# Hybrid attention block: key tile 3 of the stick-breaking heads in two fp32r products, the last 16 keys in one stacked product, three merge gates ahead of the first branch product

## The chip, the core and the metric

The kernel runs on one core of a Trainium2 chip. The metric is the device time of one execution in microseconds (us). The engines are named as in the profile: PE (TensorE, matrix products; PEld are its weight loads), DVE (VectorE), ACT (ScalarE), POOL (GpSimd), SP (SyncE, which issues most DMAs). SBUF is the on-chip memory, PSUM the accumulators that PE writes.

## What is computed

One decoder block on 512 tokens of width 1024, with 16 meta tokens put in front (L = 528): a layer norm, one wide projection, eight differential attention heads, sixteen stick-breaking heads, a SiLU gate on each, two branch products merged by sigmoid gates, an output projection, and a residual with layer norm. Cut to what the change touches:

```python
proj = jnp.einsum('bld,dn->bln', h, w_in[i])
q_d, k_d, v_d, g_d, q_s, k_s, v_s, g_s, m_d, m_s = jnp.split(proj, IN_OFFSETS, axis=-1)

# differential head: ALiBi bias, two softmaxes, a = p0 - lam * p1
s = jnp.einsum('bhcqd,bhckd->bhcqk', q, k) * (DIFF_HEAD_DIM ** -0.5)
p = jax.nn.softmax(jnp.where(dist >= 0, s + alibi, -jnp.inf), axis=-1)
a = p[:, :, 0] - lam * p[:, :, 1]
y_d = jnp.einsum('bhqk,bhkd->bhqd', a, v)

# stick-breaking head
z = jnp.einsum('bhqd,bhkd->bhqk', q, k) * (SB_HEAD_DIM ** -0.5)
log_keep = jnp.where(before, jax.nn.log_sigmoid(-z), 0.0)
suffix = lax.cumsum(log_keep, axis=3, reverse=True) - log_keep
a = jnp.where(before, jnp.exp(jax.nn.log_sigmoid(z) + suffix), 0.0)
y_s = jnp.einsum('bhqk,bhkd->bhqd', a, v)

br_d = jnp.einsum('blw,wd->bld', y_d * jax.nn.silu(g_d), w_br_diff[i])
br_s = jnp.einsum('blw,wd->bld', y_s * jax.nn.silu(g_s), w_br_sb[i])
merged = jax.nn.sigmoid(m_d + b_gate[i, 0]) * br_d + jax.nn.sigmoid(m_s + b_gate[i, 1]) * br_s
y = jnp.einsum('bld,de->ble', merged, w_out[i])
```

## The kernel before

**Two forms of a product.** Most fp32 operands are split into a rounded high part and the rest, both of type fp32r, and a product is the sum of two or three fp32r products, one pass over the array each (high by high, high by low, low by high). Operands that stay plain fp32 need no split and one product, which the profile lists as two passes.

**Stages.** After the start (layer norm, the normed input transposed into `hTh` and `hTl`), the work runs in 16 units: eight differential heads ("d"), then eight pairs of stick-breaking heads ("s", heads c = 0 and 1 of a pair). While a unit's attention runs, PE projects keys, values and queries of the units after it (`proj_pos` L370, `proj_tok` L356 to L358) and in the s units also two gates. Weights come as 512 KB blocks, each split into `wh` (ACT, L97) and `wl` (DVE, L103) two projections ahead, in the order of the list `seq`. A d unit takes some 24 us, an s unit some 38 us.

**One head.** Scores (`logits`, L495 and L501) go to two PSUM slots. In a stick-breaking head DVE adds a mask to the score in PSUM (L639), ACT takes two sigmoids (L642, L643), DVE runs a scan and a product into `apad` (L645, L646). The four query tiles see 144, 272, 400 and 528 keys. `transposed` turns the attention matrix on PE (L514, L519) in three PSUM tiles, and ACT and DVE split it (L524, L525) into `ta[0]` to `ta[2]`: 512, 416 and 288 query columns for key tiles 0 to 2. Key tile 3 (160 columns, `ta[3]`) and the last 16 keys (32 columns, `ta[4]`) are copied as plain fp32. `values` (L471 to L487) turns the values likewise: `V` for tiles 0 to 2, `vf` for tile 3, `v4` for the last 16.

**Products with the values.** A differential head (`d_values`) has three fp32r products for each of tiles 0 to 2 and one fp32 product each for tile 3 (L598) and the last keys (L599). In a stick-breaking head (`s_values`) the high and the low part of the 64 value columns stand side by side in the 128 stationary columns of `V[c]`, so one product gives both halves, and two products (high and low attention) do for a tile: L654 and L661 for tile 0, L659 and L660 for tiles 1 and 2. The fp32 products of tile 3 (L655) and of the last keys (L656) have 64 stationary columns. The two halves are then added (L663, L664).

**The merge.** When the units are done, both gated results are split into `ghd`, `gld`, `ghs`, `gls` (16 casts on ACT, L728, 16 subtractions on DVE, L729). Then, for each of eight output blocks: a merge gate or two (`merge_gate`, a projection of `hTh`/`hTl`), the two branch products, and the merging. Before block 0, the merge gates (0,0), (1,0) and (0,1) run in the last unit, and (1,1) and (0,2) in the loop ahead of the first branch product. The loads of `eg`, `eb` and `hr` and the work on them (L748 to L754) are written behind the loop.

**What sets the order.** The functions hand out steps with nominal times; a scheduler then orders the instructions on each engine, by its own model and the tiles' dependences. On the chip each engine runs its list in order, so the first instruction that waits holds up all behind it.

Of the kernel before, what the change touches and what calls it, by code (L numbers as in the profile page):

```python
# [16 lines left out]
P = 128  # L17
# [26 lines left out]
def hybrid_block_kernel(ctx: ExitStack, tc: tile.TileContext, x, meta, emb_g, emb_b, w_in, b_gate,  # L44
# [127 lines left out]

    dist = const.tile([P, L], F32, name="dist")
    g.iota(dist, pattern=[[-1, L]], base=400, channel_multiplier=1, allow_small_or_imprecise_dtypes=True)
    g.affine_select(dist, dist, pattern=[[-1, L]], compare_op=ALU.is_ge, fill=1e30, base=400, channel_multiplier=1)
# [237 lines left out]
    with tc.tile_pool(name="att", bufs=1) as ap:  # L413
# [6 lines left out]
        v4s = []  # L420
        for n in range(2):
            v4 = ap.tile([P, P], F32, name=f"v4{n}")
            g.memset(v4, 0.0)
            v4s.append(v4)
# [41 lines left out]
        def values(unit, kind, parity):  # L466
# [19 lines left out]
            pe.transpose(t4[:M, :P], vT[:, 512:528], ident)  # L486
            v.tensor_copy(v4[:M], t4[:M, :P])  # L487
            unit["V"] = V, vf, v4

# [21 lines left out]
        def transposed(ta, a):  # L511
# [9 lines left out]
            def split(t, w, n):  # L521
                h = ap.tile([P, w], F32R, tag=f"ah{n}", name=f"ah{n}")
                l = ap.tile([P, w], F32R, tag=f"al{n}", name=f"al{n}")
                s.copy(h, t[:, :w])  # L524
                v.tensor_tensor(l, t[:, :w], h.bitcast(F32), op=ALU.subtract)  # L525
                return h, l
# [7 lines left out]
            def part1():  # L534
# [6 lines left out]
                ta[4] = ap.tile([P, 32], F32, tag="af4", name="af4")  # L541
                s.copy(ta[4], t1[:, 416:448])

            def part2():
# [7 lines left out]
                ta[3] = ap.tile([P, 160], F32, tag="af3", name="af3")  # L552
# [287 lines left out]
```

## Time and profile before

| | us |
|---|---|
| runs: median (lowest, highest of 3) | 752.0 (751.91, 752.81) |
| profiled execution | 751.83 |
| its span, first to last instruction | 750.1 |

The profile shows one execution. The table below is its page's view of busy time and the number of instructions of the engines.

| engine | busy us | instructions |
|---|---|---|
| PE | 733.0 | 4390 |
| PEld | 651.4 | 4390 |
| DVE | 543.7 | 1181 |
| ACT | 413.2 | 983 |
| POOL | 85.2 | 106 |

How to read the rows that follow in the prediction. A row of the timeline gives start and length in us, engine, line of the code, operation, tiles written and read, for a matmul "rows*columns" of the stationary operand and the shape that streams, and a count where rows are merged; in brackets stands idle time of the engine before the row and what ended it. A row of a group gives the count, then busy time in all and the mean of one in ns, then idle time before. A row of the windows gives the stretch, its length, the busy time of PE, PEld, DVE, ACT and POOL, then the granted clock, the DMA share and GB/s. The mean clock granted to PE was 0.993.

### The profile page before, as it was taken

To read this page: it belongs to the slowest core of one execution; us is meant where nothing else is said; L and a number is where in the kernel's file an instruction comes from. 1 tells how busy PE (TensorE), PEld (TensorE's weight loads), DVE (VectorE), ACT (ScalarE), POOL (GpSimd) and SP (SyncE) were. 2 spreads that over 40 slices of the span, in tenths; PEclk is the share of its full clock that TensorE was granted. 3 is DMA by queue.
4 is the path that set the end of the run, shared out by engine and by line. 5 is a ranking of instruction groups with operands and counts; after the bars stand their busy time and mean duration, and the time that the engine had idled before them with its cause. 6 is when DMAs were issued, how large, how long until landed. Compare 5 with 4: busy or idle time off the path is not lost.

```text
span 750.1 us, 11849 instructions
## 1 busy us (share of the span) xinstructions
PE 733.0 (98%) x4390; PEld 651.4 (87%) x4390; DVE 543.7 (72%) x1181; ACT 413.2 (55%) x983; POOL 85.2 (11%) x106
## 2 busy tenths in 40 slices
PE   7999999999999999999999999999999999999996
PEld 6899999999999979898989898988878888888885
DVE  6888898888887789695969596967478343335555
ACT  6476777676777787575647474746473232324200
POOL 5510110111000000000000000001001000000101
PEclk8999999999999999999999999999999999999998
DMA  8132112121212121212222222122244333325221
GB/s 260 32 114 85 57 57 85 57 81 51 68 57 86 56 85 39 75 57 85 57 84 58 84 57 85 57 86 57 84 168 142 110 87 102 95 85 195 86 85 57
DMA packets 105340, 63.90 MB, mean 85 GB/s; under 512 B 2065, under 2 KB 100530, under 8 KB 105282
## 3 DMA queue, kind: packets, MB, share of 16 engines
q1 hardware_dynamic: 104098, 58.93, 26.6%
q10 hardware_dynamic: 1184, 4.20, 1.6%
q8 instruction: 35, 0.57, 0.3%
q14 instruction: 23, 0.19, 0.1%
HBM read 61.03 MB, written 2.10 MB: 84 GB/s over the span
## 4 chain that ended last, share of the span: by engine, by line
PE 90%; DVE 5%; ACT 3%; DMA 1%; issue 1%; POOL 0%; SPq 0%; DVEq 0%; ACTq 0%; POOLq 0%
PE ps L370 23%; PE ps L357 14%; PE ps L358 14%; PE ps L356 14%; PE sc L501 5%; PE t L514 3%; PE pso L782 2%; PE pso L781 2%; PE pso L780 2%; PE t L519 1%; PE av L659 1%; DMA raw<-in_w_in_dram 1%; PE tv L471 1%; PE av L655 1%; DVE hTl L239 1%
## 5 line engine op out<-in xcount | busy, mean ns | idle before, releaser
L103 DVE TENSOR_TENSOR wl<-raw,wh 128x512 fp32r<-128x512 f32 x187 | 131.5, 732 | 63.5 <-ACT wh L97 63.3
L97 ACT CAST wh<-raw 128x512 fp32r<-128x512 f32 x192 | 109.8, 621 | 120.8 <-PE ps L357 111.0
L370 PE MATMUL ps<-hTh,wh 128*128 128x264 f32 x512 | 147.5, 288 | 0.5 <-ACT k L452 0.4
L370 PE MATMUL ps<-hTl,wh 128*128 128x264 f32 x512 | 146.4, 286 | 0.0
L370 PE MATMUL ps<-hTh,wl 128*128 128x264 f32 x512 | 146.3, 286 | 0.0
L356 PE MATMUL ps<-hTh,wh 128*128 128x512 f32 x368 | 144.7, 393 | 0.0
L357 PE MATMUL ps<-hTl,wh 128*128 128x512 f32 x368 | 144.4, 392 | 0.0
L358 PE MATMUL ps<-hTh,wl 128*128 128x512 f32 x368 | 144.3, 393 | 0.0
L370 PEld LDWEIGHTS ps<-hTh,wh 128*128 128x128 f32 x512 | 96.5, 188 | 2.6 <-ACT k L452 0.9
L370 PEld LDWEIGHTS ps<-hTl,wh 128*128 128x128 f32 x512 | 96.6, 189 | 1.1
L370 PEld LDWEIGHTS ps<-hTh,wl 128*128 128x128 f32 x512 | 96.5, 188 | 0.0
L358 PEld LDWEIGHTS ps<-hTh,wl 128*128 128x128 f32 x368 | 69.1, 188 | 13.9
L357 PEld LDWEIGHTS ps<-hTl,wh 128*128 128x128 f32 x368 | 69.2, 188 | 13.2
L356 PEld LDWEIGHTS ps<-hTh,wh 128*128 128x128 f32 x368 | 69.2, 188 | 13.0
L645 DVE TENSOR_TENSOR_SCAN om<-om 128x528 f32<-128x528 f32 (+2 forms) x64 | 55.1, 868 | 9.9 <-ACT om L642 9.1
L501 PE MATMUL sc<-k,A 128*128 128x264 f32 (+2 forms) x256 | 54.1, 305 | 0.0
L525 DVE TENSOR_TENSOR al<-t,ah 128x512 fp32r<-128x512 f32 (+2 forms) x72 | 39.7, 571 | 19.5 <-PE av L661 12.2
L524 ACT CAST ah<-t 128x512 fp32r<-128x512 f32 (+2 forms) x72 | 34.8, 504 | 17.1 <-PE t L514 16.6
L642 ACT ACTIVATE om<-sc 128x264 f32<-128x264 f32 (+3 forms) x80 | 31.7, 397 | 21.1 <-DVE sc L639 20.2
L501 PEld LDWEIGHTS sc<-k,A 128*128 128x128 f32 x256 | 39.7, 189 | 2.5
L514 PE MATMUL t<-ident,apad 128*128 128x128 f32 x240 | 40.9, 272 | 0.7 <-DVE apad L646 0.7
L583 ACT ACTIVATE e<-e,mn 128x528 f32<-128x528 f32 (+3 forms) x64 | 37.0, 578 | 8.1 <-DVE mn L579 7.6
(210 smaller groups left out, 1340.3 us busy)
## 6 DMA issues: line engine op xcount, KB each, us to landing
raw<-in_w_in_dram SPq DMA_DIRECT2D x80, 512.0 KB, 3.8
raw<-in_w_br_diff_dram SPq DMA_DIRECT2D x8, 512.0 KB, 3.7
raw<-in_w_br_sb_dram SPq DMA_DIRECT2D x8, 512.0 KB, 3.8
rawo<-in_w_out_dram SPq DMA_DIRECT2D x8, 512.0 KB, 3.5
hr<-in_x_dram ACTq DMA_DIRECT2D x4, 512.0 KB, 6.8
out_dram<-hr SPq DMA_DIRECT2D x8, 256.0 KB, 2.0
xt<-in_x_dram SPq DMA_DIRECT2D x3, 512.0 KB, 8.8
xt<-in_x_dram SPq DMA_DIRECT2D x2, 256.0 KB, 3.4
```

Source lines behind the costliest of these rows:

```text
L97: s.copy(split[n][0][:, o, :], raws[n][:, o, :])
L103: eng.tensor_tensor(wl[:, o, :], raws[n][:, o, :], wh[:, o, :].bitcast(F32), op=ALU.subtract)
L356: pe.matmul(ps, wh[:, k, :], hh[:, k, o:], start=(k == 0), stop=False)
L357: pe.matmul(ps, wh[:, k, :], hl[:, k, o:], start=False, stop=False)
L358: pe.matmul(ps, wl[:, k, :], hh[:, k, o:], start=False, stop=(k == KT - 1))
L370: pe.matmul(ps[:, :H2], a[:, k, :], b[:, k, ts(c, H2)], start=(k == 0 and m == 0), stop=(k == KT - 1 and m == 2))
L501: pe.matmul(ps[:, :n], q, K[:, m, k0:k0 + n], start=(m == 0), stop=(m == 1))
L514: pe.transpose(t[:, o:o + P], a[:, AOFF[i] + j * P:AOFF[i] + (j + 1) * P], ident)
L524: s.copy(h, t[:, :w])
L525: v.tensor_tensor(l, t[:, :w], h.bitcast(F32), op=ALU.subtract)
L583: s.activation(e[c], e[c], AF.Exp, scale=-1.0, bias=m[:, 0:1], accum_out=zs[:, i, c:c + 1])
L645: v.tensor_tensor_scan(rev, rev, rev, 1.0, ALU.mult, ALU.min)
```

## The change

**Stick-breaking heads, key tile 3.** `V[c]` gets a fourth tile of 128 keys, `vf` goes away; the 160 columns of attention are split like the others (`ta[3]` is a pair), and the loop over tiles in `s_values` runs over 1 to 3. The fp32 product becomes two fp32r products.

**The last 16 keys, all heads.** Instead of `v4` and `af4` in fp32, there are stacked fp32r tiles: in `a4` the high part of the 16 attention rows stands in rows 0 to 15 and the low part in rows 32 to 47 (for d heads the high part again in rows 64 to 79), in `v4` the matching parts of the values, zeros between. One fp32r product over 128 rows sums them. `tails` holds a pair of tiles for the d heads and one for each c, cleared once.

**Merge gates.** `MERGE` lists them by block: (1,1), (0,2), (1,2) ahead of the first branch products, then two a block up to block 5, none for blocks 6 and 7. The list of weights follows it.

**Biases.** The distance matrix `dist` is no longer kept: the bias of head 0 is built in place, and each later bias is half the one before it.

```diff
+    MERGE = [[(1, 1), (0, 2), (1, 2)]] + [[(0, j + 2), (1, j + 2)] for j in range(1, 6)] + [[], []]
     for j in range(8):
-        seq += [(m, i) for m, i in (("ms", j + 1), ("md", j + 2)) if i < 8]
+        seq += [("m" + "ds"[c], i) for c, i in MERGE[j]]
         seq += [("bd", j), ("bs", j)]
...
+        tails = {}
+        for n in ("d", 0, 1):
+            tails[n] = (ap.tile([P, P], F32R, name=f"v4{n}"), ap.tile([P, 32], F32R, name=f"a4{n}"))
+            for t in tails[n]:
+                g.memset(t.bitcast(F32), 0.0)
...
-            V = [ap.tile([P, 3, P], F32R, tag=f"v{c}", name=f"V{c}") for c in range(2)]
-            vf = ap.tile([P, P], F32, tag="vf", name="vf")
-            v4 = v4s[parity]
+            V = [ap.tile([P, 4, P], F32R, tag=f"v{c}", name=f"V{c}") for c in range(2)]
+            t4 = ptp.tile([P, 512], F32, tag="tp", name="t4")[:M, :P]
+            pe.transpose(t4, vT[:, 512:528], ident)
             if kind == "d":
...
+                v4 = tails["d"][0]
+                s.copy(v4[:M], t4)
+                s.copy(v4[32:32 + M], t4)
+                v.tensor_tensor(v4[64:64 + M], t4, v4[:M].bitcast(F32), op=ALU.subtract)
             else:
                 for c, own, oth in ((0, LO, HI), (1, HI, LO)):
-                    src = tvv[:, :3, own]
+                    src = tvv[:, :, own]
                     s.copy(V[c][:, :, own], src)
                     v.tensor_tensor(V[c][:, :, oth], src, V[c][:, :, own].bitcast(F32), op=ALU.subtract)
-            s.copy(vf, tvv[:, 3, :])
-            t4 = ptp.tile([P, 512], F32, tag="tp", name="t4")
-            pe.transpose(t4[:M, :P], vT[:, 512:528], ident)
-            v.tensor_copy(v4[:M], t4[:M, :P])
+                    v4 = tails[c][0]
+                    s.copy(v4[:M, own], t4[:, own])
+                    s.copy(v4[32:32 + M, own], t4[:, own])
+                    v.tensor_tensor(v4[:M, oth], t4[:, own], v4[:M, own].bitcast(F32), op=ALU.subtract)
...
-                ta[4] = ap.tile([P, 32], F32, tag="af4", name="af4")
-                s.copy(ta[4], t1[:, 416:448])
+                a4, t4 = tails[head][1], t1[:M, 416:448]
+                s.copy(a4[:M], t4)
+                if head == "d":
+                    s.copy(a4[64:64 + M], t4)
+                v.tensor_tensor(a4[32:32 + M], t4, a4[:M].bitcast(F32), op=ALU.subtract)
...
-                ta[3] = ap.tile([P, 160], F32, tag="af3", name="af3")
-                s.copy(ta[3], t2[:, 288:448])
+                if head == "d":
+                    ta[3] = ap.tile([P, 160], F32, tag="ah3", name="af3")
+                    s.copy(ta[3], t2[:, 288:448])
+                else:
+                    ta[3] = split(t2, 160, 3, 288)
...
-            g.tensor_scalar(bias, dist, -(2.0 ** -(h + 1)), None, op0=ALU.mult)
+            if h == 0:
+                g.iota(bias, pattern=[[-1, L]], base=400, channel_multiplier=1, allow_small_or_imprecise_dtypes=True)
+                g.affine_select(bias, bias, pattern=[[-1, L]], compare_op=ALU.is_ge, fill=1e30, base=400,
+                                channel_multiplier=1)
+            g.tensor_scalar(bias, biases[-1] if h else bias, 0.5 if h else -0.5, None, op0=ALU.mult)
...
             pe.matmul(av, V[c][:, 0, :], ta[0][0], start=True, stop=False)
-            pe.matmul(av[own, QOFF[3]:], vf[:, own], ta[3], start=False, stop=False)
-            pe.matmul(av[own, QOFF[4]:], v4[:, own], ta[4], start=False, stop=False)
-            for j in range(1, 3):
+            pe.matmul(av[:, QOFF[4]:], v4, a4, start=False, stop=False)
+            for j in range(1, 4):
                 o = av[:, QOFF[j]:]
                 pe.matmul(o, V[c][:, j, :], ta[j][0], start=False, stop=False)
                 pe.matmul(o, V[c][:, j, :], ta[j][1], start=False, stop=False)
...
     for j in range(8):
-        run([merge_gate(c, i) for c, i in ((1, j + 1), (0, j + 2)) if i < 8])
+        run([merge_gate(c, i) for c, i in MERGE[j]])
```

**The order, place 1: PE, end of a stick-breaking head.** `av` is the head's result in PSUM, `V` its values, `ah` and `al` the split attention, `af` and `vf` the fp32 ones. Before, the products stand in one run:

```order
L655 MATMUL av<-af_5306,vf 64x160
L656 MATMUL av<-af_5291,v_506 64x32
L659 MATMUL av<-ah_5287,V_5000 128x416
L660 MATMUL av<-al_5288,V_5000 128x416
L659 MATMUL av<-ah_5302,V_5000 128x288
L660 MATMUL av<-al_5303,V_5000 128x288
L661 MATMUL av<-al_5275,V_5000 128x512
```

After, the last products of a head; the products of the last keys (`av<-a_510,v_509 128x32`) and of tile 1 stand some 20 projection products further up:

```order
L680 MATMUL av<-ah_4046,V_3738 128x288
L355 MATMUL ps<-hTh,wl 128x512
L367 MATMUL ps<-hTh,wh 128x264
L367 MATMUL ps<-hTl,wh 128x264
L681 MATMUL av<-al_4047,V_3738 128x288
L680 MATMUL av<-ah_4050,V_3738 128x160
L367 MATMUL ps<-hTh,wl 128x264
L681 MATMUL av<-al_4051,V_3738 128x160
L682 MATMUL av<-al_4019,V_3738 128x512
```

The fp32 products with 64 columns are gone, tile 3 comes as two products of 160 columns behind tile 2, and projections stand between them, as each waits for its own split.

**Place 2: DVE, scores of the first head of the fourth stick-breaking unit,** up to the mask of the score of 144 keys (`sc<-sc,om 128x144`), which frees a score slot. `wl` is a weight split, `k` the keys of the next unit, `V` and `v` the values. Before:

```order
L451 TENSOR_TENSOR k_4536<-ps,k_4536 64x264
L645 SCALAR_TENSOR_TENSOR om<-om 128x272
L453 CAST k_4536<-k_4536 64x264
L646 TENSOR_TENSOR apad_496<-sgm,om 128x271
L103 TENSOR_TENSOR wl<-raw,wh 128x512
L508 TENSOR_TENSOR om<-sc,neg 128x144
L103 TENSOR_TENSOR wl<-raw,wh 128x512
L451 TENSOR_TENSOR k_4535<-ps,k_4535 64x264
L639 TENSOR_TENSOR sc<-sc,om 128x144
```

After:

```order
L666 SCALAR_TENSOR_TENSOR om<-om 128x272
L685 TENSOR_TENSOR ysT<-av,half 64x512
L667 TENSOR_TENSOR apad_491<-sgm,om 128x271
L488 TENSOR_TENSOR V_4624<-tv,V_4624 128x4x64
L492 TENSOR_TENSOR v_505<-t_4625,v_505 16x64
L513 TENSOR_TENSOR om<-sc,neg 128x144
L449 TENSOR_TENSOR k_4594<-ps,k_4594 64x264
L104 TENSOR_TENSOR wl<-raw,wh 128x512
L660 TENSOR_TENSOR sc<-sc,om 128x144
```

The addition of the last head's halves (`ysT`), a wider split of the values and the small subtraction for the last keys have come in; one split of weights and one of the keys' subtractions less stand ahead of the mask.

**Place 3: DVE, between the last unit and the merge.** `gld`, `gls` are the low parts of the gated results, `sm` the first merged product, `hr` the residual rows, `wl` the next weights. Before:

```order
L664 TENSOR_TENSOR ysT<-av,half 64x512
L729 TENSOR_TENSOR gld<-ydT,ghd 128x512 x8
L729 TENSOR_TENSOR gls<-ysT,ghs 128x512 x4
L739 TENSOR_TENSOR sm_6429<-ps,sm_6429 128x512
L729 TENSOR_TENSOR gls<-ysT,ghs 128x512 x4
L753 SCALAR_TENSOR_TENSOR hr<-hr,xmv,eg 128x1024
L103 TENSOR_TENSOR wl<-raw,wh 128x512 x3
L753 SCALAR_TENSOR_TENSOR hr<-hr,xmv,eg 128x1024
L103 TENSOR_TENSOR wl<-raw,wh 128x512
```

After:

```order
L685 TENSOR_TENSOR ysT<-av,half 64x512
L750 TENSOR_TENSOR gld<-ydT,ghd 128x512 x8
L750 TENSOR_TENSOR gls<-ysT,ghs 128x512 x6
L774 SCALAR_TENSOR_TENSOR hr<-hr,xmv,eg 128x1024
L750 TENSOR_TENSOR gls<-ysT,ghs 128x512
L760 TENSOR_TENSOR sm_6528<-ps,sm_6528 128x512
L750 TENSOR_TENSOR gls<-ysT,ghs 128x512
L774 SCALAR_TENSOR_TENSOR hr<-hr,xmv,eg 128x1024
L104 TENSOR_TENSOR wl<-raw,wh 128x512 x2
```

One `hr` has moved ahead of the last two `gls`, and two of them stand ahead of the first `wl` instead of one. On PE, 22 projection products stand between the last product with the values and the first one with `ghd`, where there were 11; and 52 products further on, as before, comes the first one with that `wl`.

More of the change, by code (lines that the diff above doesn't have):

```diff
@@ L170, in hybrid_block_kernel @@
     hTl = hpool.tile([P, KT, 48 + L], F32R, tag="hTl", name="hTl")[:, :, 48:]
-    dist = const.tile([P, L], F32, name="dist")
-    g.iota(dist, pattern=[[-1, L]], base=400, channel_multiplier=1, allow_small_or_imprecise_dtypes=True)
-    g.affine_select(dist, dist, pattern=[[-1, L]], compare_op=ALU.is_ge, fill=1e30, base=400, channel_multiplier=1)
     neg = const.tile([P, M + P], F32, name="neg")
@@ L419, in hybrid_block_kernel @@
             apads.append(a)
[L420 to L424, printed above, removed]
+        tails = {}
[3 more added lines that the diff above has]
+                g.memset(t.bitcast(F32), 0.0)
         def stage_q(unit, kind, n):
@@ L464, in stage_v, with values @@
             unit["vT"] = vT
-        def values(unit, kind, parity):
+        def values(unit, kind):
             vT = unit["vT"]
@@ L509, in with_lo, with transposed @@
             return t
-        def transposed(ta, a):
+        def transposed(ta, a, head):
             def full(t, o, i, j):
@@ L551, in part2 @@
                 ta[2] = split(t2, 288, 2)
-                ta[3] = ap.tile([P, 160], F32, tag="af3", name="af3")
-                s.copy(ta[3], t2[:, 288:448])
+                if head == "d":
[3 more added lines that the diff above has]
+                    ta[3] = split(t2, 160, 3, 288)
             return [part0, part1, part2]
+        biases = []
         def d_scores(unit, h):
@@ L562, in d_scores @@
             bias = ap.tile([P, L], F32, tag="bias", name="bias", bufs=2)
-            g.tensor_scalar(bias, dist, -(2.0 ** -(h + 1)), None, op0=ALU.mult)
+            if h == 0:
[3 more added lines that the diff above has]
+            g.tensor_scalar(bias, biases[-1] if h else bias, 0.5 if h else -0.5, None, op0=ALU.mult)
+            biases.append(bias)
             a = apads[h % 2]
@@ L593, in d_values @@
         def d_values(unit, ta):
-            (vh, vl), vf, v4 = unit["V"]
+            (vh, vl), vf = unit["V"]
+            v4, a4 = tails["d"]
             av = pav.tile([P, 512], F32, tag="av", name="av")
@@ L598, in d_values @@
             pe.matmul(av[:, QOFF[3]:], vf, ta[3], start=False, stop=False)
-            pe.matmul(av[:, QOFF[4]:], v4, ta[4], start=False, stop=False)
+            pe.matmul(av[:, QOFF[4]:], v4, a4, start=False, stop=False)
             for j in range(1, 3):
@@ L650, in s_values @@
         def s_values(unit, c, p, ta):
-            V, vf, v4 = unit["V"]
+            V = unit["V"]
+            v4, a4 = tails[c]
             own, oth = ((LO, HI), (HI, LO))[c]
@@ L654, in s_values @@
             pe.matmul(av, V[c][:, 0, :], ta[0][0], start=True, stop=False)
-            pe.matmul(av[own, QOFF[3]:], vf[:, own], ta[3], start=False, stop=False)
-            pe.matmul(av[own, QOFF[4]:], v4[:, own], ta[4], start=False, stop=False)
-            for j in range(1, 3):
+            pe.matmul(av[:, QOFF[4]:], v4, a4, start=False, stop=False)
+            for j in range(1, 4):
                 o = av[:, QOFF[j]:]
@@ L692, in hybrid_block_kernel @@
                 proj.append(stage_q(units[u + 2], *UNITS[u + 2]))
-            steps = pending + [(0.6, lambda unit=unit: values(unit, kind, u % 2))]
+            steps = pending + [(0.6, lambda unit=unit: values(unit, kind))]
             pending = []
@@ L697, in hybrid_block_kernel @@
                 steps += spread(d_scores(unit, n), 0.0, TD[0], 10)
-                parts = transposed(ta, apads[n % 2])
+                parts = transposed(ta, apads[n % 2], "d")
                 steps += [(TD[1] + 0.7 * m, f) for m, f in enumerate(parts)]
@@ L713, in hybrid_block_kernel @@
                     steps += spread(s_scores(unit, c), 4.4 * c + (2.0 if n == 0 and c == 0 else 0.0), 0.85, 5)
-                    parts = transposed(ta, apads[c])
+                    parts = transposed(ta, apads[c], c)
                     steps += [(7.0 + 6.5 * c + 0.7 * m, f) for m, f in enumerate(parts)]
```

15 lines of the change are left out of this document (9 added, 6 removed).

## The prediction

> **What bounds the kernel now.** I read the page first: busy shares, then the chain that ended last.
>
> ```profile
> span 750.1 us, 11849 instructions
> PE 733.0 (98%) x4390; PEld 651.4 (87%) x4390; DVE 543.7 (72%) x1181; ACT 413.2 (55%) x983; POOL 85.2 (11%) x106
> ...
> PE 90%; DVE 5%; ACT 3%; DMA 1%; issue 1%; POOL 0%; SPq 0%; DVEq 0%; ACTq 0%; POOLq 0%
> ```
>
> TensorE is busy for 98% of the span and carries 90% of the chain. Next I asked for the busy time of one stick-breaking unit (two heads, between two value transposes); the columns after the length are PE, PEld, DVE, ACT, POOL.
>
> ```profile
> 318.00:356.00 38.00, 38.00 (x242) 33.99 (x241) 29.36 (x60) 22.99 (x60) 2.84 (x2) 1.00 0.24 70
> ```
>
> PE fills all 38.00 us; DVE has 8.6 us to spare, ACT 15. So the time is the sum of what PE streams, plus a few holes. Durations of matmuls overlap in these rows, so I price a matmul by the distance from its start to the next start.
>
> **Products with the values, stick-breaking heads.** These are the rows of PE's timeline around one head's end: start, length, line, tiles, shape, count.
>
> ```profile
> 385.01 0.39 PE L358 MATMUL ps<-hTh,wl 128*128 128x512 f32 x1
> 385.23 0.39 PE L356 MATMUL ps<-hTh,wh 128*128 128x512 f32 x1
> 385.55 0.49 PE L655 MATMUL av<-af,vf 128*64 128x160 f32 x2
> 385.87 0.25 PE L656 MATMUL av<-af,v 128*64 128x32 f32 x2
> 386.05 0.46 PE L659 MATMUL av<-ah,V 128*128 128x416 f32 x1
> 386.35 0.35 PE L660 MATMUL av<-al,V 128*128 128x416 f32 x1
> 386.54 0.29 PE L659 MATMUL av<-ah,V 128*128 128x288 f32 x1
> ```
>
> A 512-column product takes 0.22 to 0.23 us (385.01 to 385.23), a 416-column one 0.19 (386.35 to 386.54). Without L655 and L656, L659 would start at 385.46 and L660 at 385.65; L660 started at 386.35. The two plain-fp32 products, two passes each, onto 64 output rows, cost **0.70 us a head**, entering and leaving them included. There are 16 heads: the group below counts 32, two passes each.
>
> ```profile
> L655 PE MATMUL av<-af,vf 128*64 128x160 f32 x32 | 7.8, 324 | 0.0
> ```
>
> In their place stand three single-pass products with 128 stationary columns: one of 32 columns (v4 by a4) and two of 160 (tile 3 high and low). The kernel before has no single-pass fp32r product narrower than 256 columns, so their price has to be bounded. The differential heads have a 160- and a 32-column fp32 product with 128 stationary columns, and the transposes are 128 wide:
>
> ```profile
> 77.51 0.28 PE L370 MATMUL ps<-hTh,wl 128*128 128x264 f32 x1
> 77.63 0.43 PE L598 MATMUL av<-af,vf 128*128 128x160 f32 x2
> 77.90 0.30 PE L599 MATMUL av<-af,v 128*128 128x32 f32 x2
> 78.04 0.43 PE L602 MATMUL av<-ah,V 128*128 128x416 f32 x1
> 78.31 0.35 PE L603 MATMUL av<-al,V 128*128 128x416 f32 x1
> ...
> 393.22 0.27 PE L519 MATMUL t<-turned,apad 128*128 128x128 f32 x1
> 393.32 0.27 PE L514 MATMUL t<-ident,apad 128*128 128x128 f32 x1
> 393.35 0.37 PE L501 MATMUL sc<-k,A 128*128 128x264 f32 x1
> ```
>
> From 77.63, where the 264-column product's 0.12 us end, to 78.31 is 0.68; L602 itself is worth 0.19, so the fp32 work of a differential head is 0.49 us: 0.27 for the 160 columns (77.63 to 77.90), 0.22 for the two passes of 32, or 0.11 a pass. The transposes also stand 0.10 to 0.11 apart, whatever little they stream.
> - Lower end: streaming alone. From 264 columns in 0.12 to 512 in 0.225 is 0.42 ns a column, so 160 columns take 0.08, and 32 columns take 0.03, the smallest distance shown (393.32 to 393.35). A head: 0.19.
> - Upper end: a narrow product runs no faster than fp32 in both passes, 0.27 for 160 columns, 0.11 for 32. A head: 0.65.
> - I take 0.11 for all three, the distance of the nearest short products with 128 stationary columns: 0.33 a head.
>
> So a head gains 0.70 - 0.33 = 0.37 us, 16 heads **5.9 us** (from 0.8 to 8.2).
>
> A rule of the Trainium skill would make it more: the page "TensorE: Matmul & The Clock Gate", section "Back-to-back issue gap", gives N/2.4 + 2.5 ns warm, 25 ns for the smallest. By it a head would cost an estimated 0.16 us and the 16 would gain 8.6. The trace does not follow it at 128 columns, where it says 56 ns and the transposes show 110.
>
> **Differential heads.** Tile 3 stays fp32; the last 16 keys become one pass instead of two: 0.22 to 0.11, eight heads, **0.9 us** (0 to 1.5).
>
> **What the vector engines get.** DVE rows by shape: line, tiles, shapes, count, then busy, mean ns.
>
> ```profile
> L525 DVE TENSOR_TENSOR al<-t,ah 128x288 fp32r<-128x288 f32 x24 | 10.8, 451 | 6.9 <-ACT ah L524 6.6
> L639 DVE TENSOR_TENSOR sc<-sc,neg 128x128 f32<-128x128 f32 x48 | 13.6, 289 | 2.5 <-PE sc L501 2.2
> L487 DVE COPY v<-t 16x128 f32<-16x128 f32 x16 | 4.5, 279 | 1.1 <-PE t L486 0.4
> L582 DVE TENSOR_TENSOR mn<-mn 128x1 f32<-128x1 f32 x16 | 2.4, 152 | 0.3
> ```
>
> Per stick-breaking unit DVE gains two subtractions of 160 columns (0.32 each, between 289 and 451 ns), four small ones on 16 rows (0.15 to 0.28 each), 64 more columns in each of two L483 (0.06, at the 1 ns a column between the first two rows), and loses the 0.28 of L487: **1.1 to 1.6 us**. It lies beside PE's 38 us unless the scores wait for it. The tightest place I found is a score product that needs the PSUM slot which ScalarE's second sigmoid reads, itself behind a DVE row:
>
> ```profile
> 368.86 0.29 ACT L643 ACTIVATE sgm<-sc 128x144 f32<-128x144 f32 x1
> ...
> 369.20 0.41 PE L501 MATMUL sc<-k,A 128*128 128x264 f32 x2
> ```
>
> The slot was free at 369.15 and the product started at 369.20: nothing to spare there. What DVE does ahead of that row grows by one 160-column subtraction, the wider L483 and a small subtraction, less L487: 0.32 + 0.12 + 0.2 - 0.28 = 0.4 us, and PE comes 0.37 earlier for each head; but the new order also puts a subtraction of the keys (L451) and a wl behind it. So a unit loses between 0 and 0.8 us; between these I take **0.1 us, 0.8 in eight units**, near the lower end, since the row above shows PE losing nothing with no slack at all. ACT's additions are of the size of small copies and it idles 15 us a unit: 0. A differential unit gets one small subtraction on DVE: 0. On POOL the two instructions that made `dist` leave the start, but POOL's next work there waited for DVE anyway, so nothing comes of it; the halving chain of the biases keeps one instruction per head, and clearing six small tiles is done long before their first use. `t4` now takes its PSUM slot before V is copied; the next user of a slot comes a dozen products later: 0.
>
> ```profile
> L182 POOL TENSOR_TENSOR lne<-xmv,epsr 128x1 f32<-128x1 f32 x4 | 0.8, 190 | 3.9 <-DVE xmv L206 3.8
> ```
>
> Where the heads change kind, two holes remain, filled or widened by the order of the activation-table loads. The new order has as many loads; I leave the holes as they are, 0.7 us either way.
>
> ```profile
> 263.54 0.40 PE L495 MATMUL sc<-k,A 128*128 128x288 f32 x1 [1.22 <-ACT sgm L643]
> ...
> 272.95 0.63 PE L514 MATMUL t<-ident,apad 128*128 128x128 f32 x4 [0.70 <-DVE apad L646]
> ```
>
> **The third merge gate.** Around the first branch product (L356 on ghd):
>
> ```profile
> 548.39 0.58 ACT L663 COPY half<-av 64x512 f32<-64x512 f32 x1 [3.08 <-PE av L661]
> 549.73 4.27 ACT L728 CAST ghd<-ydT 128x512 fp32r<-128x512 f32 x8 [0.76 <-DVE ysT L664]
> 550.39 5.45 DVE L729 TENSOR_TENSOR gld<-ydT,ghd 128x512 fp32r<-128x512 f32 x8 [0.69 <-ACT ghd L728]
> 550.67 0.39 PE L356 MATMUL ps<-ghd,wh 128*128 128x512 f32 x1
> 551.68 0.50 PE L357 MATMUL ps<-gld,wh 128*128 128x512 f32 x1 [0.62 <-DVE gld L729]
> ```
>
> PE should have gone on at 550.90 and went on at 551.68: a hole of 0.8 us. In the new order 22 products instead of 11 stand between the last product with the values and the first ghd, 5.0 us instead of 2.5; gld needs 3.4. The hole goes: **-0.8**. What is late next is DVE's queue. Before, DVE and PE met like this:
>
> ```profile
> 554.39 0.45 ACTq L752 DMA_DIRECT2D hr<-in_x_dram  x1
> 558.89 2.49 DVE L729 TENSOR_TENSOR gls<-ysT,ghs 128x512 fp32r<-128x512 f32 x4
> 561.29 1.27 DVE L753 SCALAR_TENSOR_TENSOR hr<-hr,xmv,eg 128x1024 f32<-128x1024 f32 x1
> 562.49 1.88 DVE L103 TENSOR_TENSOR wl<-raw,wh 128x512 fp32r<-128x512 f32 x3
> 563.44 0.40 PE L358 MATMUL ps<-hTh,wl 128*128 128x512 f32 x1
> ...
> hr<-in_x_dram ACTq DMA_DIRECT2D x4, 512.0 KB, 6.8
> ```
>
> The wl half was ready at 563.1, its product started at 563.44: almost nothing to spare. In the new order one hr stands ahead of the last two gls and a second ahead of wl, and the first waits for its load with gls, the sm product and gls queued behind it. Counted from the end of av (548.3): 14 subtractions at 0.67 from +2.1 end at +11.5; hr, issued at about +6.1, lands 6.8 later at +12.9 and is done at +14.1; gls, sm, gls, hr (0.6, 0.6, 0.6, 1.2) end at +17.1, the first wl at +17.8. PE wants it 52 products after +5.0, at +16.8. **+1.0** (0 if the load is there when DVE comes, 2 if it lands a microsecond later).
>
> **Sum**, against the profiled execution's 751.83 us (span 750.1): -5.9 - 0.9 + 0.8 - 0.8 + 1.0 = -5.8, 746.0. The median of the runs is 0.2 above it: **746.2**.
>
> **Rivals.**
> 1. *Narrow fp32r products at the fp32 rate* (0.27 for 160 columns). For it: no row shows a narrow one, and everything split before is 256 wide or more. Against it: the passes of L598 stand 0.135 apart, and a single-pass product has half of them. Gain 0.8 + 0.9 - 0.8 - 0.2 = 0.7: **751.3**. 15%.
> 2. *Narrow products bound by streaming alone*: 8.2 + 1.5 - 0.8 - 0.2 = 8.7: **743.3**. This is the outcome that the page's gap formula, named above, would nearly give; the transposes speak against it. 7%.
> 3. *DVE becomes the bound of the stick-breaking units* (slower). Each split makes DVE wait for ACT's cast, and all of it, with what is left over from the head before, can come ahead of the row that frees the score slot; there is no slack there, so past the 0.1 counted every microsecond stalls PE in 8 units. For it: DVE ran without a gap in the first part of the units and the whole addition is 1.1 to 1.6 us. Against it: 8.6 us of DVE idle in the same unit, and an order that moves other rows behind. The gain is eaten at 0.1 + 5.8/8 = 0.8 us a unit; with 1.1 us the time is 746.2 + 8 x 1.0 = **754.2**. 8%, some of it short of that.
> 4. *The gate only moves its hole*: the late wl takes 2 us instead of 1, **747.2**; it is inside the forecast.
>
> **Chances and range.** Forecast (744.3 to 748.3) 70%, rival 1 15%, rival 2 7%, rival 3 8%. The range 743.0 to 751.5 takes in the ends of the narrow products' price and leaves out rival 3 and the far parts of rivals 1 and 2, under 20%. Within 0.2%, about what a measurement of this kernel can tell from no change, is 750.5 to 753.5. Faster: forecast, rival 2, a quarter of rival 1, a little of rival 3: 0.82. Same: the rest of rival 1 and the mild cases of rival 3: 0.12. Slower: 0.06.
>
> **What would show it.** In PE's timeline after, the 160-column products of the stick-breaking heads should stand 0.11 from the next start; 0.27 means rival 1, 0.08 rival 2. Fp32 rows onto 64 output rows should be gone. L356 on ghd to L357 on gld should be 0.23 apart, with a hole of about 1 us at the first hTh,wl product behind the first ghs ones, released by DVE wl. PE waits on DVE or ACT at the scores of each unit would speak for rival 3. The forecast is wrong if a unit shortens by less than 0.4 us.

## The result and the profile after

| | before | changed |
|---|---|---|
| median of 6 runs each, us (lowest, highest) | 752.4 (751.83, 752.9) | 746.37 (745.67, 746.73) |
| profiled execution, us | 751.83 | 746.5 |
| its span, us | 750.1 | 744.7 |
| PE busy, us | 733.0 | 727.7 |
| DVE busy, us | 543.7 | 549.4 |
| ACT busy, us | 413.2 | 420.2 |

The ratio of the runs is 0.9922, with a 95% interval from 0.9912 to 0.9932: the change saves 6.0 us, and the forecast was 746.2. That the total came out does not yet say that its terms did. First the page's busy time, then the windows view of the same 38 us of one stick-breaking unit as before (length, then PE, PEld, DVE, ACT, POOL).

```profile
PE 727.7 (98%) x4366; PEld 648.9 (87%) x4366; DVE 549.4 (74%) x1229; ACT 420.2 (56%) x1031; POOL 87.2 (12%) x110
```

```profile
318.00:356.00 38.00, 38.00 (x245) 34.45 (x244) 32.20 (x67) 24.51 (x65) 3.60 (x2) 1.00 0.24 70
```

PE still fills the unit; DVE has gone from 29.36 to 32.20 us of the 38 and bounds nothing. Next PE's timeline of the changed kernel, at one stick-breaking head: the product of the last keys (L677), then the first product of tile 3 (L680, 160 columns).

```profile
379.39 0.18 PE L677 MATMUL av<-a,v 128*128 128x32 f32 x1
379.42 0.44 PE L680 MATMUL av<-ah,V 128*128 128x416 f32 x1
379.70 0.35 PE L681 MATMUL av<-al,V 128*128 128x416 f32 x1
...
384.29 0.23 PE L680 MATMUL av<-ah,V 128*128 128x160 f32 x1
384.36 0.43 PE L355 MATMUL ps<-hTh,wl 128*128 128x512 f32 x1
384.63 0.39 PE L353 MATMUL ps<-hTh,wh 128*128 128x512 f32 x1
```

The 160-column product is followed after 0.07, which by the prediction's own sign ("0.08 means rival 2") would be streaming alone. But the row behind it gives part of that back: L355 is followed after 0.27, where a 512-column product takes 0.23. Over the two, 0.34 less 0.23 is 0.11. The 32 columns show it more strongly: 0.03 to the next start, and then 0.28 for 416 columns that are worth 0.19; together 0.12. **The price of a short product is read over it and the product behind it.** So a head pays 0.12 + 2 x 0.11 = 0.34 where it paid 0.70: 0.36 less, 5.8 us for 16 heads. The differential heads, in the same view:

```profile
79.14 0.44 PE L619 MATMUL av<-af,vf 128*128 128x160 f32 x2
79.31 0.29 PE L620 MATMUL av<-a4d,v4d 128*128 128x32 f32 x1
79.44 0.43 PE L623 MATMUL av<-ah,V 128*128 128x416 f32 x1
79.71 0.35 PE L624 MATMUL av<-al,V 128*128 128x416 f32 x1
```

From 79.14 to 79.71, less the 0.19 of L623, is 0.38, where it was 0.49: 0.11 less, 0.9 us for eight heads. At the first branch product PE's timeline now reads:

```profile
551.57 0.39 PE L355 MATMUL ps<-hTh,wl 128*128 128x512 f32 x1
551.80 0.39 PE L353 MATMUL ps<-ghd,wh 128*128 128x512 f32 x1
552.02 0.39 PE L354 MATMUL ps<-gld,wh 128*128 128x512 f32 x1
...
563.36 0.39 PE L355 MATMUL ps<-ghs,wl 128*128 128x512 f32 x1
563.58 0.39 PE L355 MATMUL ps<-hTh,wl 128*128 128x512 f32 x1
```

L353 to L354 is 0.22: the hole of 0.8 is gone. The hole of 1.0 that the prediction put at the first hTh,wl product behind the ghs ones is not there either: it starts at 563.58, 0.22 behind the product before it. DVE's timeline at that place:

```profile
554.66 3.69 DVE L750 TENSOR_TENSOR gls<-ysT,ghs 128x512 fp32r<-128x512 f32 x6
558.27 1.27 DVE L774 SCALAR_TENSOR_TENSOR hr<-hr,xmv,eg 128x1024 f32<-128x1024 f32 x1
...
561.39 1.28 DVE L774 SCALAR_TENSOR_TENSOR hr<-hr,xmv,eg 128x1024 f32<-128x1024 f32 x1
562.58 1.29 DVE L104 TENSOR_TENSOR wl<-raw,wh 128x512 fp32r<-128x512 f32 x2
```

DVE began the first hr at 558.27 without waiting, 5.85 us behind its issue, which ACT's timeline has:

```profile
552.42 0.82 ACTq L773 DMA_DIRECT2D hr<-in_x_dram  x2
```

### The profile page after: what moved, and what is told of

It is laid out like the page before. It is cut to its first block, busy times and chain, and to the rows that moved or that the text cites. A ratio compares the mean times of both kernels' runs of the same rounds, so it can differ in the third digit from the quotient of the medians.

```text
span 744.7 us, 11916 instructions
## 1 busy us (share of the span) xinstructions
PE 727.7 (98%) x4366; PEld 648.9 (87%) x4366; DVE 549.4 (74%) x1229; ACT 420.2 (56%) x1031; POOL 87.2 (12%) x110
## 4 chain that ended last, share of the span: by engine, by line
PE 88%; DVE 5%; ACT 3%; DMA 1%; issue 1%; POOL 0%; SPq 0%; DVEq 0%; POOLq 0%
PE ps L367 22%; PE ps L353 15%; PE ps L354 15%; PE ps L355 15%; PE sc L506 4%; PE t L519 3%; PE pso L802 2%; PE pso L801 2%; PE pso L803 2%; PE t L524 1%; DMA raw<-in_w_in_dram 1%; PE av L680 1%; PE tv L469 1%; PE av L681 1%; DVE hTl L236 1%
## 5 line engine op out<-in xcount | busy, mean ns | idle before, releaser
L104 DVE TENSOR_TENSOR wl<-raw,wh 128x512 fp32r<-128x512 f32 x187 | 129.6, 722 | 71.7 <-ACT wh L98 71.4
L353 PE MATMUL ps<-hTh,wh 128*128 128x512 f32 x368 | 144.9, 394 | 0.0
L354 PE MATMUL ps<-hTl,wh 128*128 128x512 f32 x368 | 144.5, 393 | 0.0
L355 PE MATMUL ps<-hTh,wl 128*128 128x512 f32 x368 | 144.1, 392 | 0.0
L355 PEld LDWEIGHTS ps<-hTh,wl 128*128 128x128 f32 x368 | 69.1, 188 | 13.9
L354 PEld LDWEIGHTS ps<-hTl,wh 128*128 128x128 f32 x368 | 69.2, 188 | 13.7
L353 PEld LDWEIGHTS ps<-hTh,wh 128*128 128x128 f32 x368 | 69.1, 188 | 12.9 <-ACT vT L461 0.2
L506 PE MATMUL sc<-k,A 128*128 128x264 f32 (+2 forms) x256 | 56.7, 310 | 0.1
L529 ACT CAST ah<-t 128x512 fp32r<-128x512 f32 (+2 forms) x88 | 39.1, 467 | 20.2 <-DVE al L530 10.8
L530 DVE TENSOR_TENSOR al<-t,ah 128x512 fp32r<-128x512 f32 (+2 forms) x88 | 45.0, 527 | 3.7 <-ACT ah L529 3.2
L519 PE MATMUL t<-ident,apad 128*128 128x128 f32 x240 | 42.5, 272 | 0.0
```

The costliest lines, as they stand in the source:

```text
L104: eng.tensor_tensor(wl[:, o, :], raws[n][:, o, :], wh[:, o, :].bitcast(F32), op=ALU.subtract)
L353: pe.matmul(ps, wh[:, k, :], hh[:, k, o:], start=(k == 0), stop=False)
L354: pe.matmul(ps, wh[:, k, :], hl[:, k, o:], start=False, stop=False)
L355: pe.matmul(ps, wl[:, k, :], hh[:, k, o:], start=False, stop=(k == KT - 1))
L506: pe.matmul(ps[:, :n], q, K[:, m, k0:k0 + n], start=(m == 0), stop=(m == 1))
L519: pe.transpose(t[:, o:o + P], a[:, AOFF[i] + j * P:AOFF[i] + (j + 1) * P], ident)
```

## The experiments

Each kernel's median is set against the kernel before as run beside it; where two kernels of different sets are compared, both ratios are given.

**The changed kernel again.**

> The changed kernel once more, for a second profile of it. Ratio to the kernel before 0.992 (746.4 us against 752.4). The first product with hTh started at 13.61 us in the first profile of the changed kernel and at 12.69 in that of the kernel before, behind the load of the second x tile. If that 0.9 us belongs to the change (two POOL instructions fewer ahead of the loads' users), it stands at 13.6 again; if it is the loads of that one execution, it stands anywhere from 12.6 to 13.7.

745.75 us against 752.12, ratio 0.9911 [0.9898, 0.9925]. The first product with hTh started at 13.03. It waits for the layer norm of the second x tile, and this for its load. DVE's rows of the kernel before and of the first profile of the changed one:

```profile
6.94 1.29 DVE L202 BATCH_NORM_STATS2 lnst<-xt 128x6 f32<-128x512 f32 x2 [1.09 <-DMA xt<-in_x_dram]
```

```profile
8.05 1.29 DVE L199 BATCH_NORM_STATS2 lnst<-xt 128x6 f32<-128x512 f32 x2 [2.24 <-DMA xt<-in_x_dram]
```

In the second profile of the changed kernel, the same kernel once more, that row starts at 7.36: between two executions of one kernel it moved by 0.7 us. In the twelve profiles with the changed start the first hTh product came between 12.64 and 13.70 us, in the two with the start of before at 12.69 and 13.15. The late load of the first profile (0.9 us) is within what the loads do from one execution to the next; a small part that belongs to the change is not excluded by two profiles.

**What a narrow product costs.** Two kernels add 32 products each, one with as many columns again, one with none. In narrow_twice:

```diff
-            for j in range(1, 4):
+            for j in (1, 2, 3, 3):
```

and in narrow_halved:

```diff
+                for k in (0, 80) if j == 3 else (0,):
+                    w = 80 if j == 3 else 512 - QOFF[j]
+                    o = av[:, ds(QOFF[j] + k, w)]
+                    pe.matmul(o, V[c][:, j, :], ta[j][0][:, ds(k, w)], start=False, stop=False)
+                    pe.matmul(o, V[c][:, j, :], ta[j][1][:, ds(k, w)], start=False, stop=False)
```

> Both 160-column products of tile 3 in the stick-breaking heads are issued twice (32 more products; tile 3 then counts double in the output). Theory A, a narrow product holds PE 0.113 us, 0.074 to the next start and 0.04 by which the one after that is late: +32 x 0.113 = +3.6 us over the changed kernel, 750.0. Theory B, it costs the distance to the next start alone: +32 x 0.074 = +2.4 us, 748.8. Theory C, the fp32 rate of rival 1 (0.27): +8.6 us, 755.

> Each 160-column product of tile 3 is issued as two of 80 columns: 32 more products, not one column more. Theory A, the price goes by the product, about 0.11 however narrow: +3.6 us over the changed kernel, 750.0. Theory B, it goes by the columns: 0, 746.4.

Twice: 748.44 us, ratio 0.9950 [0.9937, 0.9962], 2.7 us over the changed kernel of this set. Halved: 749.04 us, ratio 0.9956 [0.9944, 0.9969], 3.3 over it. Both profiled spans are 747.3, 3.1 over 744.2, or 0.10 for each of the 32 products. The first rise lies between theories A and B (3.6 and 2.4) and could not have told them apart; the second rules out B: 80 columns cost what 160 do. PE's timeline of the kernel with halves:

```profile
385.10 0.20 PE L683 MATMUL av<-al,V 128*128 128x80 f32 x1
385.14 0.27 PE L682 MATMUL av<-ah,V 128*128 128x80 f32 x1
385.24 0.28 PE L683 MATMUL av<-al,V 128*128 128x80 f32 x1
385.35 0.48 PE L684 MATMUL av<-al,V 128*128 128x512 f32 x1
385.67 0.27 PE L524 MATMUL t<-turned,apad 128*128 128x128 f32 x1
```

The first of three is followed after 0.04, the next two after 0.10 and 0.11, and the 512 columns behind them take 0.32 instead of 0.23: 0.57 - 0.23 = 0.34 for three, 0.11 each.

**Which part of the 0.36 a head.** In tile3_fp32 tile 3 is back in fp32 on 64 columns:

```diff
+            pe.matmul(av[own, QOFF[3]:], vf[:, own], ta[3], start=False, stop=False)
-            for j in range(1, 4):
+            for j in range(1, 3):
```

In tail_fp32 the last keys are, and tile 3 stays split:

```diff
-            pe.matmul(av[:, QOFF[4]:], v4, a4, start=False, stop=False)
+            pe.matmul(av[own, QOFF[4]:], v4[:, own], a4, start=False, stop=False)
```

fp32_128 is tile3_fp32 with the values in 128 columns, the other head's half zero:

```diff
-            pe.matmul(av[own, QOFF[3]:], vf[:, own], ta[3], start=False, stop=False)
+            pe.matmul(av[:, QOFF[3]:], vf[c], ta[3], start=False, stop=False)
```

> The changed kernel with key tile 3 of the stick-breaking heads back in plain fp32 on 64 columns; the stacked last keys and the three gates stay. Theory A, tile 3 carries most of the 0.36 us a head: a head pays about 0.55 (two passes at 0.19 and 0.14, and going into the 64 columns and out of them some 0.1 each) in place of 0.226, 16 x 0.33 = 5.2, less 0.5 of waits for DVE that go with the split: +4.7 us over the changed kernel, 750.5. Theory B, most of the gain was the stacking of the last keys: +2 us or less, 747.7.

> The changed kernel with the last 16 keys of the stick-breaking heads back in plain fp32 on 64 columns, and tile 3 in its two fp32r products: the fourth case beside both in fp32 (0.70 us a head for the narrow products), only the last keys stacked (0.70 as well: 5.9 us for 16 heads over the changed kernel) and both changed (0.34). Theory A, what is dear is one visit to fp32 with 64 columns, in and out, whatever is done there: a head pays 0.226 and some 0.33 for the visit, +0.22 x 16 = +3.5 us over the changed kernel, 749.2. Theory B, all of the gain belongs to tile 3: 0 to +0.5 us, 746.

> The kernel tile3_fp32 (tile 3 of the stick-breaking heads in plain fp32, last keys stacked, 751.17 us, 0.725 us a head for the narrow products), with one difference: the fp32 values of tile 3 stand in 128 stationary columns, the other head's 64 columns zero, so that the product goes onto all 128 rows of the accumulator. Theory A, what is dear is changing to 64 columns and back (0.09 ahead, 0.19 and 0.23 for the two passes, 0.11 behind): a head then pays what a differential head pays in the changed kernel, 0.385, and the time falls by 16 x 0.34 = 5.4 us to 745.7, as fast as the changed kernel without splitting tile 3 at all. Theory B, plain fp32 is dear on any number of columns: no gain, 751.2.

PE's timelines, one head of each; first tile3_fp32:

```profile
309.80 0.39 PE L353 MATMUL ps<-hTh,wh 128*128 128x512 f32 x1
310.11 0.49 PE L681 MATMUL av<-af,vf 128*64 128x160 f32 x2
310.53 0.46 PE L684 MATMUL av<-ah,V 128*128 128x416 f32 x1
310.83 0.35 PE L685 MATMUL av<-al,V 128*128 128x416 f32 x1
```

then tail_fp32:

```profile
312.54 0.39 PE L355 MATMUL ps<-hTh,wl 128*128 128x512 f32 x1
312.86 0.30 PE L676 MATMUL av<-a,v 128*64 128x32 f32 x2
313.09 0.46 PE L679 MATMUL av<-ah,V 128*128 128x416 f32 x1
313.39 0.35 PE L680 MATMUL av<-al,V 128*128 128x416 f32 x1
```

and fp32_128:

```profile
308.06 0.39 PE L353 MATMUL ps<-hTh,wh 128*128 128x512 f32 x1
308.29 0.43 PE L685 MATMUL av<-af,vf 128*128 128x160 f32 x2
308.45 0.46 PE L688 MATMUL av<-ah,V 128*128 128x416 f32 x1
308.74 0.35 PE L689 MATMUL av<-al,V 128*128 128x416 f32 x1
```

In the first, from 309.80 to 310.83, less 0.23 for L353 and 0.19 for L684, 0.61 goes to tile 3. In the second, from 312.54 to 313.39 with the same taken off, 0.43 goes to the last keys. In the third, from 308.06 to 308.74, 0.26 goes to the same two fp32 passes of 160 columns as in the first. With the other part's price:

| kernel | tile 3, us a head | last keys | sum | median us | ratio to before |
|---|---|---|---|---|---|
| before | both fp32, 64 columns | | 0.70 | | |
| tile3_fp32 | fp32, 64: 0.61 | stacked: 0.11 | 0.72 | 751.17 | 0.9988 [0.9980, 0.9997] |
| tail_fp32 | fp32r: 0.23 | fp32, 64: 0.43 | 0.66 | 749.52 | 0.9966 [0.9954, 0.9977] |
| changed | fp32r: 0.22 | stacked: 0.12 | 0.34 | 745.75 | 0.9911 [0.9898, 0.9925] |
| fp32_128 | fp32, 128: 0.26 | stacked: 0.11 | 0.37 | 744.89 | 0.9908 [0.9893, 0.9924] |

Neither part alone saves more than 0.04 a head; together they save 0.36. What was dear was the change to 64 columns and back, paid once a head, and paid in full while one product still asks for it: 0.61 and 0.43 for the two alone make 1.04, where both together cost 0.70, so that some 0.34 is common to them. And fp32 by itself was not the reason: on 128 columns, with zeros in the other half, tile 3 costs nearly what the split costs. Whether an fp32r product on 64 columns would be as dear is not shown, as none was run. This kernel has the lowest median of all, with 545.8 us of DVE instead of 549.4; its interval overlaps the changed kernel's, so it is not shown to be faster, only as fast with less work.

**Is DVE near its limit?**

```diff
-                v.tensor_tensor(l, t[:, o:o + w], h.bitcast(F32), op=ALU.subtract)
+                for _ in range(3 if w == 160 else 1):
+                    v.tensor_tensor(l, t[:, o:o + w], h.bitcast(F32), op=ALU.subtract)
```

> The changed kernel with the low part of tile 3 subtracted three times over in each stick-breaking head (2 x 0.32 us more of DVE a head, 10 us in all; the result is the same). Theory A, DVE's idle time and the planned order take nearly all of it: 0 to +1.5 us over the changed kernel, 745.8 to 747.3. Theory B, rival 3, DVE is close to the bound of the units: +1.3 a unit, +10 us, 756.

```profile
PE 729.2 (98%) x4366; PEld 650.4 (87%) x4366; DVE 559.3 (75%) x1261; ACT 420.3 (56%) x1031; POOL 87.5 (12%) x110
```

745.38 us, ratio 0.9918 [0.9904, 0.9931]: 9.9 us more of DVE than the 549.4 of the changed kernel, and no time lost. Rival 3 is refuted.

**The third gate, taken away and given to the kernel before.**

```diff
-    MERGE = [[(1, 1), (0, 2), (1, 2)]] + [[(0, j + 2), (1, j + 2)] for j in range(1, 6)] + [[], []]
+    MERGE = [[(c, i) for c, i in ((1, j + 1), (0, j + 2)) if i < 8] for j in range(8)]
```

> The changed kernel with the merge gates in the order of the kernel before (two ahead of the first branch product). Theory A, the third gate removed a hole of 0.8 us ahead of gld and cost nothing in its place: 0.8 to 1.0 us over the changed kernel, 747.3, with the hole of 0.8 back between ghd and gld in PE's timeline. Theory B, as the prediction had it, the third gate also brings a late wl of 1.0 us, which this run would be rid of: -0.2 us, 746.2.

> The kernel before with nothing but the third merge gate moved ahead. Theory A, the gate's worth depends on what stands behind the last product with the values: here 11 products stood there already and the hole is 0.8 us, so the gate is worth 0.8 to 1.0: 751.3 us against 752.1. Theory B, the gate is worth in any kernel what it is worth in the changed one (6.2 us, 751.97 without it against 745.75): 746. Of the start: this kernel has the start of the kernel before; if its first product with hTh comes at 12.7 us again, the later start of the changed kernel (13.0 to 13.6 in five profiles) belongs to the change; anything from 13.0 on speaks for the loads of the one execution.

gates_two: 751.97 us, ratio 0.9999 [0.9990, 1.0008]. Without the third gate the change saves nothing at all; both theories were off by five microseconds. before_gates_three: 751.37 us, ratio 0.9995 [0.9986, 1.0005]: there the gate is worth 0.3, not told from nothing, though its profile shows the hole gone:

```profile
556.55 0.39 PE L357 MATMUL ps<-ghd,wh 128*128 128x512 f32 x1
556.77 0.39 PE L358 MATMUL ps<-gld,wh 128*128 128x512 f32 x1
```

PE's timeline of gates_two shows why, with the windows view of the stretch behind it (the granted clock is the third number from the end):

```profile
545.61 0.43 PE L682 MATMUL av<-al,V 128*128 128x512 f32 x1
548.88 0.49 PE L353 MATMUL ps<-ghd,wh 128*128 128x512 f32 x1 [2.85 <-ACT ghd L749]
550.14 0.50 PE L354 MATMUL ps<-gld,wh 128*128 128x512 f32 x1 [0.76 <-DVE gld L750]
...
551.29 0.63 PE L355 MATMUL ps<-ghd,wl 128*128 128x512 f32 x1
551.71 0.63 PE L353 MATMUL ps<-ghd,wh 128*128 128x512 f32 x1
```

```profile
551.00:554.40 3.40, 3.40 (x10) 2.62 (x9) 3.40 (x7) 3.40 (x7) 0.00 (x0) 0.50 0.80 266
```

In the new order nothing stands behind the last product with the values: PE waits until `half`, `ysT`, ghd and gld have been made one after the other. In the order of before there were 11 projection products at this place, with the third gate 35; in the changed kernel there are 22 with the gate and none without. The first ghd product comes 3.0 us later than it could (545.61 to 548.88, less 0.23), gld another 1.0 (548.88 to 550.14, less 0.23), and then the products stand up to 0.43 apart in place of 0.23 while the granted clock is 0.50: nine products take 3.65 us (550.94 to 554.59) in place of 2.05, 1.6 more. That is 5.6 of the 5.8 us between the two profiled spans (750.0 and 744.2).

The Trainium skill ("TensorE: Matmul & The Clock Gate", "Part 1: The HAM clock gate (the "warmup" mystery)") says that the clock falls to one half after an idle window of about 3.4 us and comes back after as long a busy one, the windows running free. This trace agrees in the length of the slow stretch: 0.50 from 551.0 to 554.4, 3.4 us with PE busy throughout. It shows no idle window of 3.4 us ahead of it: PE stood still for 2.85 and then for 0.76 us, and the clock fell only when PE had been at work again for 0.9 us. Two kernels tried to keep the clock up by products into an unused accumulator behind `half`. gates_two_warm does it in fp32 on 64 rows:

```diff
+                for k in range(5):
+                    pe.matmul(fill, ident[own], half[own], start=(k == 0), stop=(k == 4))
```

and fill_fast in one pass on 128 rows:

```diff
+                s.copy(late[:, :32], av[:, :32])
+                for k in range(8):
+                    pe.matmul(fill, V[c][:, 0, :], late, start=(k == 0), stop=(k == 7))
```

> The kernel with the two gates (751.97 us), and behind the last product with the values five fp32 products of 512 columns into an unused accumulator, which read `half`: they can start when ACT has written it (1.9 us into the wait of 3.3) and are through 2.3 us later, about when the first gld comes. In the run without them TensorE then ran at a granted clock of 0.50 for 3.3 us. Theory A, the clock fell because TensorE stood still, and half of 3.3 us is lost by it: with the fill the clock stays at 1.0 and the time falls by 1.0 to 1.7 us, to 750.6. Theory B, the clock is not the cause, since gld comes only every 0.67 us and the three products on it take 0.68 at full clock: no gain, 752.0 or a little more.

> The kernel with the two gates (751.97 us) once more with a fill behind the last product with the values, now eight single-pass products of 512 columns on all 128 rows (1.8 us) into an unused accumulator. They need a small copy of the accumulator that ACT makes behind `half`, so they stand from 1.9 to 3.7 us into the wait and ACT's first ghd comes about 0.2 later. The fill of the run before it was fp32 on 64 rows, lasted twice as long as meant, and the clock fell to 0.50 all the same. Theory A, the clock fell because TensorE did too little: with these the clock holds at 1.0 and 1.0 to 1.6 us come back, 750.6. Theory B, the first 1.6 us of standing still are enough: the clock falls to 0.50 again, 752.2.

gates_two_warm: 757.89 us, ratio 1.0085 [1.0071, 1.0098]. The fill was far too long (its ten passes took 6.3 us in the profile). The clock fell 2.6 us into it and stayed at 0.50 for 10.2 us, though PE was busy with the fill for the first 3.4 of them; the rule of the Trainium skill named above would have brought it back then. So this fill did not hold the clock, and the run does not tell what a held clock is worth. fill_fast: 752.47 us (751.16 to 754.32), ratio 1.0007 [0.9998, 1.0017]. In its profile the clock held at 1.00 and the span was 749.4 against 750.0, with the first gld product 1.2 later for the fill's sake (5.75 us behind the last product with the values, against 4.53); but over 12 runs the mean clock lay between 0.987 and 0.995, and the five runs at 0.990 or below took 752.7 to 754.3. The mean clocks suggest that with the fill the clock falls in some executions and not in others, and the median gains nothing. So the waits are shown to cost 4.0 us, and the slower clock is seen to stretch the products behind them; that the remainder can be had back by keeping TensorE busy is not shown.

**A last try at a better version**, from the hole that is left where the heads change kind (PE waits 0.8 us for ACT's sigmoid, behind four table loads):

```diff
-                pending = [(3.0 if n < 7 else 1.0, lambda unit=unit, n=n: d_norm(unit, n))]
+                pending = [(3.0 if n < 7 else 0.0, lambda unit=unit, n=n: d_norm(unit, n))]
```

> The changed kernel with one planning time changed (the norm of the last differential head, 1.0 to 0.0). On ACT its exponential then follows its logarithm with no sigmoids between, and one of the four table loads between 257 and 265 us goes. TensorE there stood still for 1.0 us for a score slot, and three times for 0.3 to 0.4. Theory A, the slot was late by that load (1.28) and the sigmoids it brought ahead: 0.5 to 1.2 us under the changed kernel, 744.8. Theory B, the wait moves to the next releaser in the same place: 745.8.

752.61 us, ratio 1.0006 [0.9997, 1.0015], where the changed kernel has 745.75 and 0.9911: 6.9 worse, and neither theory held. PE's timeline and the window behind it:

```profile
262.37 0.63 PE L519 MATMUL t<-ident,apad 128*128 128x128 f32 x4 [0.54 <-DVE V L488]
265.97 0.61 PE L500 MATMUL sc<-k,A 128*128 128x288 f32 x1 [2.97 <-ACT sgm L664]
...
268.73 0.80 PE L353 MATMUL ps<-hTh,wh 128*128 128x512 f32 x1 [1.37 <-ACT vT L461]
```

```profile
268.80:273.40 4.60, 4.60 (x11) 3.67 (x12) 3.79 (x9) 2.59 (x9) 0.00 (x0) 0.50 0.38 114
```

One table load is gone, but the three left stand close together, and the scheduler, given another time, had put the projections elsewhere: PE has nothing to do meanwhile and waits 2.97 us. The granted clock fell to 0.50 at 263.6, some 0.6 us into this wait, and came back at 273.9, 10.2 us later; the window shows 4.6 us of that with PE busy. They are the two losses of gates_two, waits and a slow clock, at another place.

## Why the prediction was right, and where it was not

Against the first profile (-5.3; by the medians -6.0), step by step:

| step | predicted | found | from |
|---|---|---|---|
| stick-breaking heads | -5.9 | -5.8 | 0.70 to 0.34 a head |
| differential heads | -0.9 | -0.9 | 0.49 to 0.38 a head |
| hole ahead of gld | -0.8 | -0.8 | rows at 551.80 and 552.02 |
| late wl behind ghs | +1.0 | 0 | row at 563.58 |
| first product with hTh | 0 | +0.9 | 12.69 to 13.61; +0.3 in the second profile |
| the rest of the units | +0.8 | +1.3 | what is left of -5.3 |

1. **The narrow products** were right in size: 0.33 a head predicted, 0.34 found. The sign that was to show it was wrong: the distance to the next start is 0.07, not 0.11, and the other 0.04 shows one row later. The reason given for the old price was incomplete. The prediction took the 0.70 as that of "two plain-fp32 products, two passes each, onto 64 output rows" and let one pass replace two; fp32_128 shows that 128 columns in place of 64 would have done nearly all of it. Rival 1 had the price of two fp32 passes of 160 columns right (0.27; fp32_128 has 0.26), and failed because a single-pass product costs 0.11; but it set that price on each of two products, and the prediction had no case in which the one fp32 product stays and only its 64 columns go, which brings some 0.33 a head (0.70 to 0.37). The gap rule of the Trainium skill ("TensorE: Matmul & The Clock Gate", "Back-to-back issue gap"), which the page gives for an isolated product, fits the distance (it gives some 0.07 for 160 columns), and not the price, which the halves show to go by the product.
2. **The differential heads** came as worked out.
3. **DVE's lateness** cannot be told apart well. The rest of +1.3 is not waiting that the profile shows: PE was not busy for 17.1 us of the span before (750.1 less 733.0) and for 17.0 after (744.7 less 727.7). The holes where the heads change kind, which the prediction left as they were, shrank: the first from 1.2 to 0.8 us, the second (0.70) is gone, and the longest other wait behind it in the units is 0.24. So the rest stands in PE's busy time, where the rows overlap and short delays do not show as waits. It is not spread as 0.1 on each unit. From the first value transpose of a unit (`tv`) to that of the next, two stick-breaking units in a row took 37.1 us each where they had taken 37.9, 0.8 less, which is all that the products save (0.7) and a little more; the unit ahead of them took 37.65 where it had taken 37.92, only 0.3 less, below the 0.4 that the prediction had named as its bound. That dve_more loses nothing says that it is not the amount of DVE's work. The step that put 0.1 on each unit for that reason is not borne out; what delays single units stays open.
4. **The late wl** was the step that failed: "hr, issued at about +6.1, lands 6.8 later". 6.8 us is not what the first hr takes from issue to landing, but the median of four loads issued one behind the other. The first landed sooner: in the kernel before, the view of DMA issues over 554.30 to 554.60 has

```profile
hr<-in_x_dram ACTq DMA_DIRECT2D x1, 512.0 KB, 6.0
```

   and in the changed kernel DVE found it there 5.85 us after the issue. Counted from the end of av (546.93 here), it was issued at +5.5 in place of +6.1, and DVE was done with this hr at +12.6 in place of +14.1, 1.5 us earlier than worked out. So wl was ready at about 563.2 for a product at 563.58.
5. **The gate** was priced against the hole of the kernel before (0.8). The prediction did count 22 products in the new order, with the gate, but not what that order has without it: the gate alone is worth 0.3 there and 6.2 here. The total was right because it was worked out on the whole new order. As a price of that edit it was wrong by five microseconds.

Two errors of opposite sign (+1.0 for wl that did not come, and the late start and rest that were left out) made the total look better than its terms; that they nearly cancel is luck.

## What to carry to other kernels

Price a short product over itself and the next long one, and look at the width of its stationary operand before its type: here one visit of fp32 to 64 columns a head cost more than splitting the operand did, and went only when the last product left them. Before a stretch where engines hand a result on one after the other, count the products that TensorE still has in the order; when an edit moves the end of a loop by a dozen products, the cover goes with it, and the wait may take the clock down too. Take edits that were made together apart in both directions, since here tile 3 alone, the last keys alone or all without the gate were worth a fraction of the 6 us that they bring together.

## What the runs showed of the hardware

- A single-pass product of 80 or 160 columns with 128 stationary columns holds PE 0.10 to 0.11 us, of which up to 0.07 shows only in the product behind it.
- Two fp32 passes of 160 columns take 0.61 us on 64 stationary columns, with the way in (0.09 longer ahead) and out, and 0.26 on 128.
- The granted clock was 0.50 for 3.4 us behind waits of 2.85 and 0.76 us (gates_two), and for 10.2 us from 0.6 us into a wait of 2.97 (norm_earlier). In gates_two_warm it fell 2.6 us into a fill of fp32 products on 64 rows that kept PE busy, for 10.2 us as well.
- In two profiles of the same kernel the load of the second x tile let DVE begin on it at 7.36 and at 8.05 us.
